# Moving the forget gate's chain of a hybrid recurrent and attention block to 128 rows, earlier in the program

## The chip, the cores and the metric

The kernel runs on one core of a Trainium2 chip. The metric is device time in microseconds for one execution, shown as the median over several. Five engines work side by side, each with its own list of instructions in a fixed order: TensorE (PE in the profile: matrix products), VectorE (DVE) and ScalarE (ACT) for elementwise work, GpSimd (POOL) and SyncE (SP). SP issues the loads of weights; POOL issues a second stream of transfers. An instruction that waits holds up everything behind it on its engine or queue.

## The reference, cut to what matters

A layer of 512 tokens and 1024 channels: a norm, one input projection, a recurrent branch (A), an attention branch with a forget gate (B), a gated sum of both, and a feed-forward part.

```python
h = rms_norm(x, mix_norm_pre[layer])
proj = jnp.einsum("bsd,de->bse", h, w_in[layer])
xa, ga, q, k, v, f_logit, g_a, g_b = jnp.split(proj, offs, axis=-1)
y_a = jax.nn.gelu(ga) * hr                       # hr: the recurrence over xa
y_b = forgetting_attention(q, k, v, f_logit + b_forget[layer])
merged = (jax.nn.sigmoid(g_a + b_merge[layer, 0]) * jnp.einsum("bse,ed->bsd", y_a, w_proj_a[layer])
          + jax.nn.sigmoid(g_b + b_merge[layer, 1]) * jnp.einsum("bse,ed->bsd", y_b, w_proj_b[layer]))
# in forgetting_attention, per head: 16 heads, 512 tokens
cum = jnp.cumsum(jax.nn.log_sigmoid(f_logit.astype(jnp.float32)), axis=1).transpose(0, 2, 1)
sc = sc + cum[:, :, qs:qe, None] - cum[:, :, None, :qe]
```

The forget gate is small: 16 logits per token, their log-sigmoid, and a running sum over the tokens. Attention needs it as a bias on its scores.

## The kernel before, in words

Precision: every product is made of three, with both operands split into a high half (a rounded copy: `wh`, `yh`, `hh`) and a low half (the rest: `wl`, `yl`, `hl`). A weight goes through three steps: SP loads it (`raw_…`), ACT rounds it (`wh_…`, L205), DVE subtracts (`wl_…`, L208). The pool `wpool` has four buffers of each kind. `unit(name)` hands out a weight and starts the ones two further on.

The stages that matter, in the order of TensorE:

- **ga**: ten products of 24 matmuls (`ga0` to `ga9`, function `project`). Their results go through GeLU and times the recurrence to `yh`, `yl` (L800 to L805).
- **pa**: the branch's output projection, sixteen loads and units of 15 matmuls (L251 to L253), here numbered 0 to 15 in the order `PA_ORDER`. Unit 3 is the first that needs the rows of `yh`, `yl` from the second half, the last of them `ga9`'s.
- **q0, k0**: the first query and key projections; then the **gates** `ma`, `mb`, sixteen tiles in eight pairs, with seven products per pair (sums of blocks of weights and activations take the place of an eighth). Their operands are sums over the normed activations: `hf` (L887 to L890), its high half `gsh` (ACT, L967) and low half `gsl` (DVE), and sums of weights `gt` with `gth`, `gtl`.

After each unit, `background` has POOL make a copy of one column of `wh` (`tick`, L182), which places the next of the background transfers (`td`, sums of blocks of the last weight matrix, through HBM) behind that unit. The buffer of `wh` is free for its next weight only when the tick has read it.

The function `forget` is called once, in `early_sums(3)`, so behind pa unit 3: its weights are split (L841 to L845), 16 matmuls make `pf` of 48 rows (L848, L849), ACT and DVE add the bias to `z` (16 rows of 512). `log1p_exp_neg` (L303 to L316) works out the log of 1 + exp(-|z|) by a series: some 14 operations of DVE and one exp on ACT. Then the running sum (`tensor_tensor_scan`, L860), the keys (L862), and four transfers to `cnd` in HBM, from where attention reads them later. Right after, `early_sums(3)` closes the pool of these tiles, and the tiles `hf` are laid into the same memory. `early_sums(6)` to `(11)` make the sums `hf`, `(12)` loads the first gate pair (`raw_ma`), `(13)` to `(15)` make its sums.

Within this part the framework's scheduler keeps the written order where operands allow it and puts ready work between; the later gate part has a schedule written by hand. On SP the loads and the chain's transfers stand in one list.

Of the kernel before, what the change touches and what calls it, by code (L numbers as in the profile page):

```python
# [8 lines left out]
F32 = mybir.dt.float32  # L9
# [3 lines left out]
ALU = mybir.AluOpType  # L13
# [3 lines left out]
P = 128  # L17
S = 512
D = 1024
KD = D // P  # L20
NT = S // P
DR = 1280
TR = DR // P
# [3 lines left out]
H = 16  # L27
# [26 lines left out]
PO = [0, 128, 384, 768, 1280]  # L54
# [43 lines left out]
def kernel(  # L98
# [15 lines left out]
    nc = tc.nc  # L114
    act, dve, pool, pe = nc.scalar, nc.vector, nc.gpsimd, nc.tensor
# [7 lines left out]
    def bank(name):  # L123
        return pspools[-1].tile([P, 512], F32, tag="ps", name=name)
# [55 lines left out]
    def background(n, w):  # L180

        i = pool.tensor_copy(out=tick, in_=w[0].bitcast(F32)[:, 0, 0:1])  # L182
        with tc.issue_after(i.ins):
            for _ in range(n):
                next(transfers, lambda: None)()
# [58 lines left out]
    def unit(name, ahead=2):  # L244

        i = where[name]
        fetch(i + ahead)
        return ready.pop(name)
# [6 lines left out]
    def project(dst, unit, ah, al, lo=0, hi=S):  # L255
        wh, wl = unit
        for k in range(KD):
            mm3(dst[:, lo:hi], wh[:, k], wl[:, k], turns(ah[:, k, lo:hi]), turns(al[:, k, lo:hi]), k == 0, k == KD - 1)
# [60 lines left out]
    mstk = ExitStack()  # L319
# [36 lines left out]
    def sub(out, a, b):  # L356
        dve.tensor_tensor(out=out, in0=a, in1=b, op=ALU.subtract)  # L357
# [173 lines left out]
    with ExitStack() as rg:  # L531
# [242 lines left out]
        def batch(ops):  # L774
            with tc.issue_after(last_act[0].ins):
                for op in ops:
                    last_act[0] = op()
# [8 lines left out]
        def rg_sqrt(t):  # L786
            return lambda: act.activation(out=tt[t], in_=tt[t], func=AF.Sqrt)
# [4 lines left out]
        def scan(t):  # L792
            dve.tensor_tensor(out=tt[t], in0=tt[t], in1=ixt[t], op=ALU.mult)
            dve.tensor_tensor_scan(out=ixt[t], data0=rt[t], data1=tt[t], initial=0.0, op0=ALU.mult, op1=ALU.add)
# [21 lines left out]
                inflow(t)  # L816
        v_out(1, pv)
        steps = {0: (range(0, 4), ()), 1: (range(4, TR), range(0, 2)), 2: ((), range(2, 5)), 3: ((), range(5, 7)), 4: ((), range(7, 9)), 5: ((), range(9, TR))}
        outs = {2: (0,), 3: (1,), 4: (2, 3), 5: (4,), 6: (5,), 7: (6, 7), 8: (8,), 9: (9,)}
        for t in range(TR):  # L820
            gas[t] = bank(f"ga{t}")
            w = unit(f"ga{t}")
            project(gas[t], w, hh, hl)
            background(2, w)
            sq, sc = steps.get(t, ((), ()))
            batch([rg_sqrt(i) for i in sq])
            for i in sc:
                scan(i)
            for i in outs.get(t, ()):
                gate_out(i)  # L830

        papool = mstk.enter_context(tc.tile_pool(name="pa", bufs=1, reuse_waits="tile"))
        pa = papool.tile([P, KD, S], F32, name="pa")
        cnd = ctx.enter_context(tc.tile_pool(name="cnd", bufs=1, space=bass.MemoryType.DRAM)).tile([H, PO[NT]], F32, name="cnd")

        def forget():
            def tl(name, n=H, dt=F32):
                return tpool.tile([P, S], dt, tag="tt", name=f"f_{name}")[0:n]

            fr = tl("fr", P)[:, : KD * H].rearrange("p (k e) -> p k e", k=KD)  # L840
            nc.sync.dma_start(fr, w_f)  # L841
            fw = tl("fw", P, F32R)[:, : KD * 48].rearrange("p (k e) -> p k e", k=KD)
            pool.memset(fw[:, :, H:32].bitcast(F32), 0.0)
            act.copy(fw[:, :, 0:H], fr)
            dve.tensor_tensor(out=fw[:, :, 32:48], in0=fr, in1=fw[:, :, 0:H].bitcast(F32), op=ALU.subtract)  # L845
            pf = bank("f")
            for k in range(KD):
                pe.matmul(pf[0:48], fw[:, k], turns(hh[:, k]), start=k == 0, stop=False)  # L848
                pe.matmul(pf[0:48], fw[:, k], turns(hl[:, k]), start=False, stop=k == KD - 1)  # L849
            z = tl("z")  # L850
            act.copy(z, pf[32:48])
            dve.scalar_tensor_tensor(out=z, in0=pf[0:H], scalar=cpt[0:H, C_BF : C_BF + 1], in1=z, op0=ALU.add, op1=ALU.add)
            with tc.issue_after(last_act[0].ins):
                l1p = log1p_exp_neg(z, tl)
            dve.tensor_scalar(out=z, in0=z, scalar1=0.0, scalar2=None, op0=ALU.min)
            dve.scalar_tensor_tensor(out=z, in0=l1p, scalar=-2.0, in1=z, op0=ALU.mult, op1=ALU.add)
            ones = tl("ones")
            pool.memset(ones, 1.0)
            cum = tl("cum")
            dve.tensor_tensor_scan(out=cum, data0=ones, data1=z, initial=0.0, op0=ALU.mult, op1=ALU.add)  # L860
            keys = tl("keys")
            dve.tensor_scalar(out=placed(keys), in0=parted(cum), scalar1=-8.0, scalar2=None, op0=ALU.mult)  # L862
            for b in range(NT):
                nc.sync.dma_start(cnd[:, PO[b] : PO[b + 1]], keys[:, : PO[b + 1] - PO[b]])

        tgpool = mstk.enter_context(tc.tile_pool(name="tg", bufs=3, reuse_waits="tile"))
        gdram = ctx.enter_context(tc.tile_pool(name="gdram", bufs=1, space=bass.MemoryType.DRAM))
# [6 lines left out]
        fq = []  # L874

        def early_sums(step):
            if step == 3:
                forget()
                rg2.close()
                gates.kpool = dstk.enter_context(tc.tile_pool(name="gkeep", bufs=2, reuse_waits="tile"))  # L880
                gates.tpool = sumstk.enter_context(tc.tile_pool(name="gsum", bufs=2, reuse_waits="tile"))
                hfpool = hfstk.enter_context(tc.tile_pool(name="hf", bufs=1, reuse_waits="tile"))
                fq.extend(hfpool.tile([P, KH, SH], F32, name=f"hf{i}") for i in range(4))
            elif 6 <= step < 10:
                i = step - 6
                k, c = (slice(0, KH), slice(KH, KD))[i % 2], (X, Y)[i // 2]
                dve.tensor_tensor(out=fq[i], in0=hh[:, k, c].bitcast(F32), in1=hl[:, k, c].bitcast(F32), op=ALU.add)  # L887
            elif step == 10:
                dve.tensor_tensor(out=fq[3], in0=fq[2], in1=fq[3], op=ALU.add)
                sub(fq[2], fq[0], fq[2])  # L890
            elif step == 11:
                sub(fq[0], fq[3], fq[0])
                sub(fq[1], fq[1], fq[0])
            elif step == 12:
                gp[0] = Pair(gates, 0, GP[0])
            elif step == 13:
                gp[0].sums(0)
                gp[0].sums(1)
            elif step == 14:
                gp[0].sums_hi(0)  # L900
                gp[0].sums_lo(0)
            elif step == 15:
                gp[0].sums_hi(1)
                gp[0].sums_lo(1)
# [881 lines left out]
```

## Time and profile before

| what | value |
|---|---|
| median of 3 runs | 884.7 us (884.02 to 884.9) |
| the profiled execution's own time | 884.92 us |
| its span in the trace | 883.1 us |
| mean granted clock of TensorE | 0.998 |
| busy: TensorE, VectorE, ScalarE, GpSimd | 868.6, 743.5, 608.4, 236.3 us |
| the 16 f matmuls | 191.2 to 194.7 us |
| the forget chain on VectorE | 195.5 to 215.4 us |
| the four cnd transfers | issued from 215.41 us |
| the sums hf begin | 221.47 us |
| q0 begins on TensorE | 233.53 us |

Times within the execution count from the start of the span. In the rows of the profile a tile's name stands without its number; `out<-in` says what is written from what; a bracket at a row's end gives the idle time before the instruction and what ended it. SPq and POOLq rows are the issues of transfers; in the list of issues the last number is the time from issue to landing.

### The profile page before, as it was taken

To read this page: it belongs to the slowest core of one execution; us is meant where nothing else is said; L and a number is where in the kernel's file an instruction comes from. 1 tells how busy PE (TensorE), PEld (TensorE's weight loads), DVE (VectorE), ACT (ScalarE), POOL (GpSimd) and SP (SyncE) were. 2 spreads that over 40 slices of the span, in tenths; PEclk is the share of its full clock that TensorE was granted. 3 is DMA by queue.
4 is the path that set the end of the run, shared out by engine and by line. 5 is a ranking of instruction groups with operands and counts; after the bars stand their busy time and mean duration, and the time that the engine had idled before them with its cause. 6 is when DMAs were issued, how large, how long until landed. Compare 5 with 4: busy or idle time off the path is not lost.

```text
span 883.1 us, 15782 instructions
## 1 busy us (share of the span) xinstructions
PE 868.6 (98%) x5856; PEld 792.3 (90%) x5856; DVE 743.5 (84%) x1209; ACT 608.4 (69%) x1031; POOL 236.3 (27%) x283
## 2 busy tenths in 40 slices
PE   9999999999999999999999999999999999999996
PEld 7888888888899998888888889999999999888884
DVE  8986479637978849998868599999999999889997
ACT  7565695532466648776754597888888888688774
POOL 4244344535411024232205100242332332100000
PEclk9999999999999999999999999999999999999999
DMA  7787689999865477453506762879899898699864
GB/s 269 242 288 207 188 214 265 227 273 196 190 148 165 120 261 274 133 173 127 203 26 203 234 200 95 192 178 241 210 222 240 209 233 210 230 384 303 280 192 147
DMA packets 71040, 185.24 MB, mean 210 GB/s; under 512 B 7153, under 2 KB 27681, under 8 KB 70578
## 3 DMA queue, kind: packets, MB, share of 16 engines
q1 hardware_dynamic: 47360, 127.72, 43.4%
q0 software_dynamic: 23456, 56.37, 29.8%
q8 instruction: 46, 0.75, 0.3%
q14 instruction: 32, 0.26, 0.1%
q10 hardware_dynamic: 146, 0.14, 0.0%
HBM read 150.69 MB, written 35.73 MB: 211 GB/s over the span
## 4 chain that ended last, share of the span: by engine, by line
PE 83%; DVE 8%; issue 4%; ACT 2%; POOL 2%; DMA 1%; DVEq 0%; ACTq 0%; POOLq 0%
PE up L464 7%; PE up L462 7%; PE up L461 7%; PE dn L1490 2%; PE dn L1488 2%; PE dn L1489 2%; PE ga L252 2%; PE ga L251 2%; PE ga L253 2%; DVE al L357 2%; PE pb L251 2%; PE xa L251 2%; PE v L341 2%; PE xa L253 2%; PE v L342 2%
## 5 line engine op out<-in xcount | busy, mean ns | idle before, releaser
L397 POOL DMA_DIRECT2D ml<-raw_up x42 | 36.1, 859 | 147.6 <-ACT ml L396 82.5
L1360 DVE SCALAR_TENSOR_TENSOR u<-up,cpt,u 128x511 f32<-128x511 f32 x96 | 71.3, 745 | 3.5 <-ACT u L1354 1.8
L1490 PE MATMUL dn<-wh_dn,al 128*128 128x512 f32 (+1 forms) x180 | 66.6, 370 | 1.3 <-DVE al L357 0.7
L1489 PE MATMUL dn<-wl_dn,ah 128*128 128x512 f32 (+1 forms) x180 | 66.1, 367 | 0.5 <-DVE wl_dn L208 0.5
L1488 PE MATMUL dn<-wh_dn,ah 128*128 128x512 f32 (+1 forms) x180 | 65.8, 366 | 0.2 <-ACT ah L1454 0.2
L461 PE MATMUL up<-sh,th 128*128 128x256 f32 x252 | 59.5, 275 | 0.0
L462 PE MATMUL up<-sl,th 128*128 128x256 f32 x252 | 59.5, 275 | 0.0
L208 DVE TENSOR_TENSOR wl_dn<-raw_dn,wh_dn 128x1024 fp32r<-128x1024 f32 x42 | 52.9, 1259 | 5.4 <-ACT wh_dn L205 5.2
L357 DVE TENSOR_TENSOR tl<-t,th 128x1024 fp32r<-128x1024 f32 x42 | 51.1, 1218 | 0.0
L1354 ACT ACTIVATE u<-up,cpt 128x512 f32<-128x512 f32 x48 | 37.0, 778 | 20.1 <-PE up L464 10.0
L205 ACT CAST wh_dn<-raw_dn 128x1024 fp32r<-128x1024 f32 x42 | 44.4, 1058 | 6.1 <-PE dn L1490 3.7
L461 PEld LDWEIGHTS up<-sh,th 128*128 128x128 f32 x252 | 48.4, 192 | 0.0
L462 PEld LDWEIGHTS up<-sl,th 128*128 128x128 f32 x252 | 48.4, 192 | 0.0
L1368 POOL TENSOR_TENSOR yf<-u,u 128x512 f32<-128x512 f32 x23 | 30.5, 1328 | 59.3 <-issue 46.5
L443 ACT CAST th<-t 128x1024 fp32r<-128x1024 f32 x42 | 43.8, 1044 | 2.4
L1490 PEld LDWEIGHTS dn<-wh_dn,al 128*128 128x128 f32 x180 | 34.1, 189 | 8.0 <-DVE al L357 4.1
L955 POOL TENSOR_TENSOR B<-B,mask 128x128 f32<-128x128 f32 x64 | 30.6, 506 | 34.8 <-DMA B<-cnd 33.7
L461 PE MATMUL up<-h2h,mh 128*128 128x256 f32 x168 | 39.7, 275 | 0.0
L462 PE MATMUL up<-h2l,mh 128*128 128x256 f32 x168 | 39.7, 275 | 0.0
L1489 PEld LDWEIGHTS dn<-wl_dn,ah 128*128 128x128 f32 x180 | 34.1, 189 | 5.8 <-DVE wl_dn L208 1.8
L1050 ACT ACTIVATE P<-P,mx 128x384 f32<-128x384 f32 (+3 forms) x64 | 35.2, 552 | 5.3 <-DVE mx L1045 4.3
L464 PE MATMUL up<-sh,tl 128*128 128x256 f32 x252 | 38.4, 275 | 0.0
(731 smaller groups left out, 3252.4 us busy)
## 6 DMA issues: line engine op xcount, KB each, us to landing
raw_up<-in_w_up_dram SPq DMA_DIRECT2D x48, 512.0 KB, 5.5
td<-in_w_down_dram POOLq DMA_DIRECT2D x36, 512.0 KB, 6.3
raw_dn<-td SPq DMA_DIRECT2D x24, 512.0 KB, 5.4
ml<-raw_up POOLq DMA_DIRECT2D x21, 512.0 KB, 5.4
B<-cnd POOLq DMA_DIRECT2D x16, 640.0 KB, 5.7
raw_dn<-in_w_down_dram SPq DMA_DIRECT2D x18, 512.0 KB, 4.4
raw_wo<-in_w_out_dram SPq DMA_DIRECT2D x16, 512.0 KB, 4.4
td<-td POOLq DMA_DIRECT2D x12, 512.0 KB, 11.2
```

The source lines that it names most:

```text
L205: act.copy(self.wh, self.raw)
L208: engine.tensor_tensor(out=self.wl, in0=self.raw, in1=self.wh.bitcast(F32), op=ALU.subtract)
L251: pe.matmul(dst, ah, bh, start=first, stop=False)
L357: dve.tensor_tensor(out=out, in0=a, in1=b, op=ALU.subtract)
L443: act.copy(self.th[i], self.t[i])
L461: pe.matmul(dst, wh[:, k], turns(ah[:, k]), start=first and k == 0, stop=False, skip_group_check=True)
L462: pe.matmul(dst, wh[:, k], turns(al[:, k]), start=False, stop=False, skip_group_check=True)
L464: pe.matmul(dst, wl[:, k], turns(ah[:, k]), start=False, stop=k == KH - 1, skip_group_check=True)
L1360: dve.scalar_tensor_tensor(out=c[:, s:], in0=ps[:, : S - s], scalar=col(C_CFW + 3 * e + j), in1=c[:, s:], op0=ALU.mult, op1=ALU.add)
L1488: pe.matmul(d[:, x], ah[:, k, tok], bh, start=first, stop=False, skip_group_check=True)
L1489: pe.matmul(d[:, x], ah[:, k, tok], bl, start=False, stop=False, skip_group_check=True)
L1490: pe.matmul(d[:, x], al[:, k, tok], bh, start=False, stop=last, skip_group_check=True)
```

## The change

`forget` becomes a generator in pieces, and two tensors in HBM, `zd` and `ld`, are added. The first piece (weights) runs in ga behind `ga5`, the matmuls and `z` behind `ga8`, the next behind `ga9`, the logarithm in `early_sums(1)`, the running sum and the keys in `early_sums(4)`. Between, `z` is written to `zd` and read back as `f_wide`: the same numbers on 128 rows of 64 columns. The series works on these, in four slices of one tile. Its result goes to `ld` and comes back as `f_zl` on 16 rows of 512, since the running sum runs along a row. The sums `hf` and the first gate pair stand one step earlier than before.

```diff
-        for t in range(TR):
-...
+        HC = P // H
+        fdram = ctx.enter_context(tc.tile_pool(name="fdram", bufs=1, space=bass.MemoryType.DRAM))
+        zd, ld = (fdram.tile([H, S], F32, name=n) for n in ("zd", "ld"))
         def forget():
...
             dve.tensor_tensor(out=fw[:, :, 32:48], in0=fr, in1=fw[:, :, 0:H].bitcast(F32), op=ALU.subtract)
+            yield
             pf = bank("f")
...
             dve.scalar_tensor_tensor(out=z, in0=pf[0:H], scalar=cpt[0:H, C_BF : C_BF + 1], in1=z, op0=ALU.add, op1=ALU.add)
-            with tc.issue_after(last_act[0].ins):
-                l1p = log1p_exp_neg(z, tl)
-            dve.tensor_scalar(out=z, in0=z, scalar1=0.0, scalar2=None, op0=ALU.min)
-            dve.scalar_tensor_tensor(out=z, in0=l1p, scalar=-2.0, in1=z, op0=ALU.mult, op1=ALU.add)
+            nc.sync.dma_start(zd, z)
             ones = tl("ones")
             pool.memset(ones, 1.0)
+            yield
+            wide = tl("wide", P).rearrange("p (n c) -> p n c", c=S // HC)
+            parts = {n: wide[:, i] for i, n in enumerate(("z", "y", "d", "s"))}
+            z2 = parts["z"]
+            nc.sync.dma_start(z2, zd.rearrange("h (n c) -> (h n) c", n=HC))
+            yield
+            with tc.issue_after(last_act[0].ins):
+                l1p = log1p_exp_neg(z2, parts.get)
+            dve.tensor_scalar(out=z2, in0=z2, scalar1=0.0, scalar2=None, op0=ALU.min)
+            dve.scalar_tensor_tensor(out=z2, in0=l1p, scalar=-2.0, in1=z2, op0=ALU.mult, op1=ALU.add)
+            nc.sync.dma_start(ld.rearrange("h (n c) -> (h n) c", n=HC), z2)
+            zl = tl("zl")
+            nc.sync.dma_start(zl, ld)
+            yield
             cum = tl("cum")
-            dve.tensor_tensor_scan(out=cum, data0=ones, data1=z, initial=0.0, op0=ALU.mult, op1=ALU.add)
+            dve.tensor_tensor_scan(out=cum, data0=ones, data1=zl, initial=0.0, op0=ALU.mult, op1=ALU.add)
...
+        fg = forget()
+        for t in range(TR):
+...
+            background(2, w)
+            if t in (5, 8, 9):
+                next(fg)
+...
         def early_sums(step):
-            if step == 3:
-                forget()
+            if step == 1:
+                next(fg)
+            elif step == 4:
+                next(fg, None)
                 rg2.close()
...
-            elif 6 <= step < 10:
-                i = step - 6
+            elif 5 <= step < 9:
+                i = step - 5
...
-            elif step == 12:
+            elif step == 11:
                 gp[0] = Pair(gates, 0, GP[0])
-            elif step == 13:
+            elif step == 12:
                 gp[0].sums(0)
                 gp[0].sums(1)
```

How the lists of the engines change is shown at two places. First VectorE around the running sum (`f_cum`), the keys and the sums `hf`. The low halves `wl_pa` before are those of units 13, 14 and 15:

```order
L860 SCALAR_TENSOR_TENSOR f_cum<-f_ones,f_z 16x512
L862 TENSOR_SCALAR f_keys<-f_cum 16x512
L208 TENSOR_TENSOR wl_pa_1_2257<-raw_pa_1_2255,wh_pa_1_2256 128x640
L208 TENSOR_TENSOR wl_pa_0_2284<-raw_pa_0_2282,wh_pa_0_2283 128x640
L887 TENSOR_TENSOR hf_2077<-hh,hl 128x1024
L887 TENSOR_TENSOR hf_2078<-hh,hl 128x1024
L887 TENSOR_TENSOR hf_2079<-hh,hl 128x1024
L887 TENSOR_TENSOR hf_2080<-hh,hl 128x1024
L208 TENSOR_TENSOR wl_pa_1_2311<-raw_pa_1_2309,wh_pa_1_2310 128x640
```

In the change the same stretch of VectorE holds the low halves of units 6 to 11:

```order
L208 TENSOR_TENSOR wl_pa_0_2067<-raw_pa_0_2065,wh_pa_0_2066 128x640
L861 SCALAR_TENSOR_TENSOR f_cum<-f_ones,f_zl 16x512
L208 TENSOR_TENSOR wl_pa_1_2114<-raw_pa_1_2112,wh_pa_1_2113 128x640
L863 TENSOR_SCALAR f_keys<-f_cum 16x512
L208 TENSOR_TENSOR wl_pa_0_2140<-raw_pa_0_2138,wh_pa_0_2139 128x640
L909 TENSOR_TENSOR hf_2108<-hh,hl 128x1024
L909 TENSOR_TENSOR hf_2109<-hh,hl 128x1024
L208 TENSOR_TENSOR wl_pa_1_2164<-raw_pa_1_2162,wh_pa_1_2163 128x640
L909 TENSOR_TENSOR hf_2110<-hh,hl 128x1024
L208 TENSOR_TENSOR wl_pa_0_2190<-raw_pa_0_2188,wh_pa_0_2189 128x640
L909 TENSOR_TENSOR hf_2111<-hh,hl 128x1024
L911 TENSOR_TENSOR hf_2111<-hf_2110,hf_2111 128x1024
```

The running sum now waits for a transfer (`f_zl`) with the low halves of units 7 and later behind it, and the sums `hf` stand ahead of unit 9's low half, where they stood ahead of unit 15's.

Second SP, from the chain's first transfer to the load of unit 10 (loads of units 7, 8, 9 and 10 among them); before, only loads stood here:

```order
L843 DMA zd<-f_z 16x512
L850 DMA f_wide<-zd 128x64
L199 DMA raw_pa_1_2112<-in_w_proj_a_dram 128x640
L199 DMA raw_pa_0_2138<-in_w_proj_a_dram 128x640
L199 DMA raw_pa_1_2162<-in_w_proj_a_dram 128x640
L856 DMA ld<-f_wide 128x64
L858 DMA f_zl<-ld 16x512
L199 DMA raw_pa_0_2188<-in_w_proj_a_dram 128x640
```

Each reading transfer waits on SP until the writing one ahead of it has landed. Further down the list, in the change, the pair `raw_ma` follows the loads of units 12 and 13 and stands ahead of those of units 14 and 15; before, it stood behind unit 14's and ahead of unit 15's.

```order
L199 DMA raw_pa_0_2239<-in_w_proj_a_dram 128x640
L199 DMA raw_pa_1_2264<-in_w_proj_a_dram 128x640
L380 DMA raw_ma_2288<-in_w_in_dram 128x1024
L380 DMA raw_ma_2289<-in_w_in_dram 128x1024
L199 DMA raw_pa_0_2293<-in_w_proj_a_dram 128x640
L199 DMA raw_pa_1_2322<-in_w_proj_a_dram 128x640
L199 DMA raw_q_2347<-in_w_in_dram 128x1024
```

The pair takes the buffers of units 10 and 11; unit 14's load takes that of unit 12, unit 15's that of 13, and q0's that of 14. A load is issued when the low half made from the buffer's last weight is done.

More of the change, by code (lines that the diff above doesn't have):

```diff
@@ L818 @@
         steps = {0: (range(0, 4), ()), 1: (range(4, TR), range(0, 2)), 2: ((), range(2, 5)), 3: ((), range(5, 7)), 4: ((), range(7, 9)), 5: ((), range(9, TR))}
-        outs = {2: (0,), 3: (1,), 4: (2, 3), 5: (4,), 6: (5,), 7: (6, 7), 8: (8,), 9: (9,)}
-        for t in range(TR):
[L821 to L833, printed above, removed]
         cnd = ctx.enter_context(tc.tile_pool(name="cnd", bufs=1, space=bass.MemoryType.DRAM)).tile([H, PO[NT]], F32, name="cnd")
+        HC = P // H
+        fdram = ctx.enter_context(tc.tile_pool(name="fdram", bufs=1, space=bass.MemoryType.DRAM))
+        zd, ld = (fdram.tile([H, S], F32, name=n) for n in ("zd", "ld"))
         def forget():
@@ L864, in forget @@
                 nc.sync.dma_start(cnd[:, PO[b] : PO[b + 1]], keys[:, : PO[b + 1] - PO[b]])
+        fg = forget()
+        outs = {2: (0,), 3: (1,), 4: (2, 3), 5: (4,), 6: (5,), 7: (6, 7), 8: (8,), 9: (9,)}
+        for t in range(TR):
+            gas[t] = bank(f"ga{t}")
+            w = unit(f"ga{t}")
+            project(gas[t], w, hh, hl)
+            background(2, w)
+            if t in (5, 8, 9):
+                next(fg)
+            sq, sc = steps.get(t, ((), ()))
+            batch([rg_sqrt(i) for i in sq])
+            for i in sc:
+                scan(i)
+            for i in outs.get(t, ()):
+                gate_out(i)
+        papool = mstk.enter_context(tc.tile_pool(name="pa", bufs=1, reuse_waits="tile"))
+        pa = papool.tile([P, KD, S], F32, name="pa")
         tgpool = mstk.enter_context(tc.tile_pool(name="tg", bufs=3, reuse_waits="tile"))
@@ L883, in early_sums @@
                 fq.extend(hfpool.tile([P, KH, SH], F32, name=f"hf{i}") for i in range(4))
-            elif 6 <= step < 10:
-                i = step - 6
+            elif 5 <= step < 9:
+                i = step - 5
                 k, c = (slice(0, KH), slice(KH, KD))[i % 2], (X, Y)[i // 2]
                 dve.tensor_tensor(out=fq[i], in0=hh[:, k, c].bitcast(F32), in1=hl[:, k, c].bitcast(F32), op=ALU.add)
-            elif step == 10:
+            elif step == 9:
                 dve.tensor_tensor(out=fq[3], in0=fq[2], in1=fq[3], op=ALU.add)
                 sub(fq[2], fq[0], fq[2])
-            elif step == 11:
+            elif step == 10:
                 sub(fq[0], fq[3], fq[0])
                 sub(fq[1], fq[1], fq[0])
+            elif step == 11:
+                gp[0] = Pair(gates, 0, GP[0])
             elif step == 12:
-                gp[0] = Pair(gates, 0, GP[0])
-            elif step == 13:
                 gp[0].sums(0)
```

## The prediction

> **What bounds the kernel now.** I read the page's first part, then the busy time by stretch, then TensorE's waits, then the timelines of VectorE (DVE), ScalarE (ACT) and the load queue SP around the change, and last how long transfers take to land.
>
> ```profile
> span 883.1 us, 15782 instructions
> PE 868.6 (98%) x5856; PEld 792.3 (90%) x5856; DVE 743.5 (84%) x1209; ACT 608.4 (69%) x1031; POOL 236.3 (27%) x283
> 186.00:215.00 29.00, 29.00 (x136) 24.32 (x136) 20.12 (x27) 10.37 (x16) 16.66 (x18) 1.00 1.00 196
> 215.00:240.00 25.00, 24.14 (x112) 20.84 (x111) 19.11 (x21) 8.66 (x12) 12.07 (x5) 1.00 0.94 207
> 240.00:252.00 12.00, 10.52 (x71) 9.68 (x71) 10.53 (x13) 8.70 (x11) 0.89 (x1) 1.00 0.59 154
> 252.00:300.00 48.00, 48.00 (x432) 48.00 (x431) 40.81 (x58) 31.77 (x53) 5.09 (x6) 1.00 0.57 155
> PE q L253 <- DVE wl_q L208: 0.9, 1, 0.9
> PE ma L461 <- DVE ma L480: 1.5, 1, 1.5
> ```
>
> TensorE (the first number after the stretch's length) is busy 98% of the span at a granted clock of 1.00 in these stretches. Where the forget chain runs today, 186 to 215, it does not idle at all. It idles only behind it: 0.9 us at the first q projection and 1.5 us at the first gate product, 2.3 us together. No change to this stretch can win more than that, 0.27%; from 252 on TensorE is full again.
>
> ```profile
> 213.68 1.21 DVE L860 TENSOR_TENSOR_SCAN f_cum<-f_ones,f_z 16x512 f32<-16x512 f32 x1
> 214.93 0.45 DVE L862 TENSOR_SCALAR f_keys<-f_cum 16x512 f32<-16x512 f32 x1
> 221.47 4.63 DVE L887 TENSOR_TENSOR hf<-hh,hl 128x1024 f32<-128x1024 f32 x4 [2.52 <-DMA cnd<-f_keys]
> 233.71 1.22 DVE L208 TENSOR_TENSOR wl_q<-raw_q,wh_q 128x1024 fp32r<-128x1024 f32 x1
> 229.04 8.20 POOL L182 COPY tick<-wh_pa 128x1 f32<-128x1 f32 x1
> 237.28 1.04 ACT L205 CAST wh_k<-raw_k 128x1024 fp32r<-128x1024 f32 x1 [2.33 <-POOL tick L182]
> 238.70 3.89 ACT L967 CAST gsh<-hf 128x1024 fp32r<-128x1024 f32 x4
> 250.19 0.43 DVE L480 TENSOR_TENSOR ma<-ma,gx 128x256 f32<-128x256 f32 x1 [1.44 <-ACT gx L468]
> ```
>
> The reader is to see one chain: the norm's sums hf start 6.1 us after the keys are done, because their memory is that of the keys, which the four cnd transfers still read. They fill DVE until wl_q at 233.71, so q waits. The tick, a copy on POOL, needs 8.2 us beside them and holds wh_k, hence gsh at 238.70, hence the add at 250.19 on which the gate product waits.
>
> **The change, part by part.** TensorE's work is the same; the sixteen f matmuls only move from behind pa unit 3 to behind ga8.
>
> ```profile
> 178.28 0.38 PE L251 MATMUL pa<-yh,wh_pa 128*128 128x512 f32 x1
> 233.53 0.38 PE L251 MATMUL q<-hh,wh_q 128*128 128x512 f32 x1
> 173.10 0.38 PE L251 MATMUL ga<-hh,wh_ga 128*128 128x512 f32 x1
> L848 PE MATMUL f<-hh,f_fw x8: 379/379/379, 191.2 to 194.3; 128*48 128x512 f32 x8
> 195.49 0.74 DVE L852 SCALAR_TENSOR_TENSOR f_z<-f,cpt,f_z 16x512 f32<-16x512 f32 x1 [2.65 <-ACT f_z L851]
> ```
>
> From 178.28 to 233.53 stand 256 matmuls of 0.216 us: a pa unit of 15 is 3.24, f is 3.45. With f first, f runs from 173.10 to 176.55, unit i (0 to 15) starts at 181.73 + 3.24 i, and q at 233.5 as now. z is ready 5.0 us after f's start (196.23 less 191.2): at 178.1.
>
> DVE saves work: twelve operations of 0.68 us and a reciprocal of 3.34 become operations on 64 columns.
>
> ```profile
> L315 DVE SCALAR_TENSOR_TENSOR lp_y_sp<-lp_y_sp,lp_d_sp x7: 155/164/201, 26.0 to 31.7; 128x10 f32<-128x10 f32 x7
> L315 DVE SCALAR_TENSOR_TENSOR f_y<-f_y,f_d x7: 673/680/697, 205.9 to 210.8; 16x512 f32<-16x512 f32 x7
> L309 DVE RECIPROCAL lp_d_sp<-lp_d_sp x1: 218/218/218, 24.0 to 24.0; 128x10 f32<-128x10 f32 x1
> L309 DVE RECIPROCAL f_d<-f_d x1: 3342/3342/3342, 198.1 to 198.1; 16x512 f32<-16x512 f32 x1
> L208 DVE TENSOR_TENSOR wl_pa<-raw_pa,wh_pa x16: 748/821/826, 166.5 to 226.0; 128x640 fp32r<-128x640 f32 x16
> L205 ACT CAST wh_pa<-raw_pa x16: 721/724/728, 165.7 to 223.2; 128x640 fp32r<-128x640 f32 x16
> ```
>
> On a straight line between 10 and 512 columns one is 0.22 us, the reciprocal 0.55. That saves some 10 us of DVE, worth nothing by itself: TensorE waited for none of it (29.00 of 29.00). What counts is that hf comes earlier, and that DVE now stands still in two new places. It can afford little: the low half wl of unit i is made when unit i-4 has left its slot, so DVE has about 3 units less 1.6 us, some 8 us of lead, and unit i needs it 0.43 us after its start (third matmul).
>
> The four new transfers and the four cnd ones go through SP's queue, among the weight loads. How long do they take?
>
> ```profile
> 41.46 0.43 SPq L199 DMA_DIRECT2D raw_v<-in_w_in_dram  x1
> raw_v<-in_w_in_dram SPq DMA_DIRECT2D x1, 512.0 KB, 8.3
> 41.98 0.56 SPq L579 DMA_DIRECT2D halo_h<-xh  x1
> halo_h<-xh SPq DMA_DIRECT2D x1, 32.0 KB, 8.0
> halo_h<-xh SPq DMA_DIRECT2D x1, 32.0 KB, 1.9
> cnd<-f_keys SPq DMA_DIRECT2D x1, 32.0 KB, 4.6
> raw_pa<-in_w_proj_a_dram SPq DMA_DIRECT2D x16, 320.0 KB, 6.1
> 174.74 0.33 SPq L199 DMA_DIRECT2D raw_pa<-in_w_proj_a_dram  x1
> raw_pa<-in_w_proj_a_dram SPq DMA_DIRECT2D x1, 320.0 KB, 8.4
> raw_ma<-in_w_in_dram SPq DMA_DIRECT2D x1, 512.0 KB, 7.0
> raw_ma<-in_w_in_dram SPq DMA_DIRECT2D x1, 512.0 KB, 6.2
> raw_q<-in_w_in_dram SPq DMA_DIRECT2D x1, 512.0 KB, 6.3
> raw_k<-in_w_in_dram SPq DMA_DIRECT2D x1, 512.0 KB, 5.2
> ```
>
> The last number of an issue row is the time to landing. A halo of 32 KB issued at 41.98 landed 8.0 us later, 0.2 behind the load issued before it (41.46 + 8.3 = 49.76): small transfers land in the queue's order. Alone (issued at 76.55) one took 1.9. So a small transfer costs 1.9 us at least, 4.6 by the nearest row of its kind (cnd), and as much as the load ahead of it where there is one; alone but beside the background transfers (DMA share 1.00 in 186 to 215) I take 3.2, the middle.
>
> [...]
>
> Now the walk. zd is issued at 178.15 behind the load of 174.74, which landed at 183.1: 183.1 (at best 180.1). wide then, nothing ahead of it: 186.3. While DVE waits, the last yl and unit 4's wl stand behind it, and exp holds four wh on ACT; all within the lead. Up to ld's source come 14 small operations and exp, taken as one more (3.3), the reciprocal (0.55), and yl, wl 4 and wl 5 (2.1, since yl runs beside exp): 192.3. ld is issued behind the loads of units 8 and 9, the latter issued at 191.6: 197.7, ld 197.9. zl: 201.2.
>
> The scan (1.2), wl 7 (0.8) and the keys (0.45) end at 203.7; unit 7 starts at 204.4, not late. hf starts 6.1 us behind the keys as now, 209.8; two hf (2.3) and wl 9 (0.8) end at 212.9, and unit 9 needs it at 211.3: **1.6 us lost.** Two more hf, their sum, and wl 10 and 11 take 5.0: 217.9. Only then the second raw_ma has a slot (its load, moved one step forward, stands before units 14 and 15): 6.6 us, the mean of 7.0 and 6.2, make 224.5. Three gate sums of half hf's size (1.8) wait for it and wl 13 (0.8) behind them: 227.1, needed at 225.9 with the loss so far: **1.2 lost.** Unit 15's load waits for wl 13's slot; at raw_k's 5.2 it lands at 232.4, wh and wl make 233.9, needed at 233.6: **0.3 lost.** raw_q has wl 14's slot at 229.8 and lands after 6.3 at 236.1; wh_q and wl_q (1.04, 1.22) end at 238.4, q starts at 236.6 and needs it at 237.1: 1.3 instead of 0.85, **0.45 lost.** wh_k no longer waits for a tick but for raw_k (239.1): wh_k starts 1.4 us before gsh as now (237.28, 238.70), so gsh at 240.5, and the add ends 11.9 us later as now (250.6 less 238.7), at 252.4. TensorE gets there at 236.6 + 1.3 + 10.4 (q and k, 48 matmuls) + 3.9 (three products of 12 matmuls half as wide) = 252.2: the 1.5 idle shrinks to 0.2, **1.3 gained.** Sum: 1.6 + 1.2 + 0.3 + 0.45 - 1.3 = +2.25 us. Span 885.35; the profiled run (884.92) would be 887.2; it lies 0.2 above the median, so 887.0 beside 884.7.
>
> The bounds: with every small transfer at 1.9 nothing is late and 2.3 is gained; with unit 9's load at 8.4 (2.3 more), zl at 4.6 (1.4 more), raw_ma at 7.0 (0.4 more), the loss is 6.3.
>
> **Rivals.** *Small transfers land at once.* If ld and cnd take 1.9 us whatever is ahead, ld's source is ready at 191.6 (ACT's table load, not wide, then ends last), zl lands at 195.6, the keys at 198.1, hf starts at 201.4, before wl 9 could be made. Every later load then has its slot when wl is made on time, wl_q is early, gsh starts right at 234: both idles go, 884.7 - 2.3 = 882.4, faster. It decides itself at hf: a start by 207.0 is enough to lose nothing at unit 13. The isolated halo speaks for it, the halos and cnd behind loads against.
>
> [...]
>
> *One loss, one gain.* If hf starts by 208.2, unit 9 is on time, but raw_ma still needs wl 11's slot (216.3): 1.2 lost at unit 13, 0.3 at 15, 0.4 at q, 1.3 gained: +0.6, 885.3. For it: my walk misses it by only 1.6 us.
>
> *Loaded queue.* If the loads ahead of ld and cnd take 8.4 as at 174.74, the upper bound: 891.0. For it: DMA share 1.00 there; against: the median of 6.1.
>
> **How the numbers follow.** Forecast 0.52, own range 885.2 to 889.5; at once 0.16; one loss 0.17; loaded 0.15. A measurement of this kernel (884.02 to 884.9) can tell about 0.2%, 1.8 us, from no change. Slower by more: 0.36 of the forecast and the loaded case, 0.51. Within: 0.16 of the forecast and 0.16 of one loss, 0.32. Faster: at once and 0.01, 0.17. The range 882.5 to 890.3 leaves out 0.1 at each end.
>
> **What would show it.** Right: TensorE waits on wl_pa (at unit 9, then 13) that do not exist now; hf with a wait on cnd of 4 us or more; the scan on zl standing from about 194 to 201; zl and cnd landing just behind weight loads; wh_k no longer behind a tick. Wrong: hf starting before 207, no wait on wl_pa, q and ma without idle; or ticks of many microseconds that hold wh_pa, which I have at nothing because DVE now has gaps.

## The result, and the profile after

The change makes the kernel slower by 0.44%: 888.8 us as median (886.9 to 889.3) beside 884.7 (882.8 to 885.9) on the same chip, ratio 1.0044 with a 95% interval of 1.0034 to 1.0054. The profiled execution took 889.16 us, its span is 887.4. The prediction was 887.0, with 882.5 to 890.3 as the range. The ratios leave out two single executions far above the others of their kernel, one of e9 (994 us) and one of e12 (3203 us).

The first part of the page of the changed kernel:

```profile
span 887.4 us, 15790 instructions
PE 870.0 (98%) x5856; PEld 792.9 (89%) x5856; DVE 734.5 (83%) x1209; ACT 607.9 (69%) x1031; POOL 220.2 (25%) x283
```

Its busy time where the forget chain ran before (after the length: TensorE, weight loads, VectorE, ScalarE, GpSimd, granted clock, share of the DMA engines, GB/s):

```profile
186.00:215.00 29.00, 26.67 (x123) 22.70 (x121) 10.46 (x25) 9.21 (x15) 9.52 (x16) 1.00 1.01 202
```

VectorE has 9.0 us less to do in all (734.5 instead of 743.5), as the change intends. But from 186 to 215, where TensorE was busy 29.00 of 29.00 us before, it now stands for 2.3 us, and VectorE, with 10.46 us of work instead of 20.12, stands too. What TensorE waits for in this part of the program:

```profile
PE pa L253 <- DVE wl_pa L208: 4.5, 2, 3.1
PE q L253 <- DVE wl_q L208: 0.3, 1, 0.3
PE ma L461 <- DVE ma L480: 0.2, 1, 0.2
```

Two waits on low halves of pa units, 4.5 us, that did not exist; the idles at q and at the first gate product are down from 0.9 and 1.5 to 0.3 and 0.2. (A further gate product now waits 0.3 us for a transfer of GpSimd's, `gml`.) VectorE's timeline shows why the low halves are late:

```profile
205.29 1.21 DVE L861 TENSOR_TENSOR_SCAN f_cum<-f_ones,f_zl 16x512 f32<-16x512 f32 x1 [10.30 <-DMA f_zl<-ld]
206.43 0.79 DVE L208 TENSOR_TENSOR wl_pa<-raw_pa,wh_pa 128x640 fp32r<-128x640 f32 x1
214.01 2.36 DVE L909 TENSOR_TENSOR hf<-hh,hl 128x1024 f32<-128x1024 f32 x2 [5.72 <-DMA cnd<-f_keys]
216.29 0.82 DVE L208 TENSOR_TENSOR wl_pa<-raw_pa,wh_pa 128x640 fp32r<-128x640 f32 x1
```

The running sum stands 10.30 us for `f_zl` with the low half of unit 7 (206.43) right behind it, and `hf` stands 5.72 us for `cnd` with that of unit 9 (216.29) behind two sums. The transfers, from the list of issues between 192 and 212 (the last number is the median time to landing):

```profile
q0 software_dynamic: 3127, 3.11, 97.6%
raw_pa<-in_w_proj_a_dram SPq DMA_DIRECT2D x4, 320.0 KB, 5.6
ld<-f_wide SPq DMA_DIRECT2D x1, 32.0 KB, 6.4
f_zl<-ld SPq DMA_DIRECT2D x1, 32.0 KB, 4.5
cnd<-f_keys SPq DMA_DIRECT2D x1, 8.0 KB, 5.4
```

The software queue, which carries the background transfers `td`, fills 97.6% of the sixteen DMA engines' time there.

**How much each place costs** is read better from the starts of matmuls than from the wait rows, since a wait row comes out shorter than what the starts show. First the idle at q of the kernel before, then the one at unit 9 of the changed kernel:

```profile
233.75 0.38 PE L252 MATMUL q<-hl,wh_q 128*128 128x512 f32 x1
234.98 0.48 PE L253 MATMUL q<-hh,wl_q 128*128 128x512 f32 x1 [0.85 <-DVE wl_q L208]
235.30 0.38 PE L251 MATMUL q<-hh,wh_q 128*128 128x512 f32 x1
```

```profile
213.64 0.38 PE L252 MATMUL pa<-yl,wh_pa 128*128 128x512 f32 x1
217.16 0.48 PE L253 MATMUL pa<-yh,wl_pa 128*128 128x512 f32 x1 [3.15 <-DVE wl_pa L208]
217.48 0.38 PE L251 MATMUL pa<-yh,wh_pa 128*128 128x512 f32 x1
```

Matmuls of 512 columns start 0.22 us apart in this part of both kernels where nothing waits. At q the third started 1.23 behind the second and the fourth 0.32 behind it: 1.11 lost, where the row says 0.85. Worked out so for each place:

| place | lost before | lost after | difference | predicted |
|---|---|---|---|---|
| unit 7 | 0 | 1.60 | +1.60 | 0 |
| unit 9 | 0 | 3.40 | +3.40 | +1.6 |
| unit 13 | 0 | 0 | 0 | +1.2 |
| unit 14 | 0 | 0.40 | +0.40 | 0 |
| unit 15 | 0 | 0 | 0 | +0.3 |
| q | 1.11 | 0.58 | -0.53 | +0.45 |
| gate product, waiting for the add | 1.75 | 0.44 | -1.31 | -1.3 |
| gate product, waiting for `gml` | 0 | 0.61 | +0.61 | 0 |
| sum | 2.86 | 7.03 | **+4.17** | **+2.25** |

The sum, from one execution of each kernel, comes close to the difference of the medians (4.1). The spans differ by 4.3; 0.94 of that is a later start-up of this one execution (the first transposes at 8.54 instead of 7.60 us, and anywhere from 0 to 0.94 later in the profiles below, whatever the kernel), and 0.8 comes back behind the gates.

So one question is settled by the trace, where the time goes; open is what makes small transfers so late, and which of the waits matters.

### The profile page after: what moved, and what is told of

It reads as the page before. It is cut to its first block, busy times and chain, and to the rows that moved or that the text cites. A ratio compares the mean times of both kernels' runs of the same rounds, so it can differ in the third digit from the quotient of the medians.

```text
span 887.4 us, 15790 instructions
## 1 busy us (share of the span) xinstructions
PE 870.0 (98%) x5856; PEld 792.9 (89%) x5856; DVE 734.5 (83%) x1209; ACT 607.9 (69%) x1031; POOL 220.2 (25%) x283
## 4 chain that ended last, share of the span: by engine, by line
PE 73%; DVE 12%; DMA 7%; issue 5%; ACT 2%; POOL 1%; SPq 0%; DVEq 0%; ACTq 0%; POOLq 0%
PE up L464 7%; PE up L461 7%; PE up L462 7%; DVE wl_dn L208 2%; DVE al L357 2%; PE ga L251 2%; PE ga L252 2%; PE ga L253 2%; PE pb L251 2%; PE v L341 2%; PE xa L251 2%; PE xa L252 2%; PE v L342 2%; PE xa L253 2%; PE v L343 2%
## 5 line engine op out<-in xcount | busy, mean ns | idle before, releaser
L205 ACT CAST wh_pa<-raw_pa 128x640 fp32r<-128x640 f32 x16 | 11.5, 723 | 39.4 <-DMA raw_pa<-in_w_proj_a_dram 24.9
```

The costliest lines, as they stand in the source:

```text
L205: act.copy(self.wh, self.raw)
```

## The experiments

Four theories at the start. **A**: the loss is VectorE standing still for the chain's transfers, with low halves queued behind. **Q**: the transfers are late because they land behind weight loads of their queue, as the prediction held. **L**: they are late because the DMA engines are loaded. **D**: the new place of the sums `hf` is what costs. All ratios are to the kernel before, run beside on the same chip.

### e1: early, but on 16 rows, without the four transfers

```diff
-            nc.sync.dma_start(zd, z)
...
-            wide = tl("wide", P).rearrange(...)
-            nc.sync.dma_start(z2, zd.rearrange(...))
...
-            nc.sync.dma_start(ld.rearrange(...), z2)
-            nc.sync.dma_start(zl, ld)
...
-            dve.tensor_tensor_scan(out=cum, data0=ones, data1=zl, ...)
+            dve.tensor_tensor_scan(out=cum, data0=ones, data1=z, ...)
```

> The change with everything in its new place, but the series on 16 rows of 512 as before, and so without zd, f_wide, ld and f_zl. Theory A (the loss is VectorE standing still for f_zl and cnd, with the low halves of units 7 and 9 queued behind): z is ready near 179, the long series and the low halves between take some 19 us, so the running sum ends near 200 instead of 206.5, cnd lands before 207, TensorE does not wait on wl_pa at unit 7 and at most 0.5 us at unit 9, and the gain at q and the first gate product stays: 883.0 to 884.5 where before is 884.7, ratio 0.998 to 1.000. Rival B (the 10 us of work that VectorE saves on 128 rows are what the early place needs): the low halves of units 4 to 7 come late behind operations of 0.68 and 3.34 us, TensorE waits on wl_pa there, ratio 1.004 or more.

Measured: 885.4 us, ratio 1.0005 (0.9996 to 1.0014). VectorE's timeline of this kernel:

```profile
201.36 1.21 DVE L853 TENSOR_TENSOR_SCAN f_cum<-f_ones,f_z 16x512 f32<-16x512 f32 x1
209.22 3.50 DVE L901 TENSOR_TENSOR hf<-hh,hl 128x1024 f32<-128x1024 f32 x3 [5.38 <-DMA cnd<-f_keys]
```

And TensorE's waits in this part (us in total, times, longest):

```profile
PE ma L461 <- DVE ma L480: 0.8, 1, 0.8
PE q L253 <- DVE wl_q L208: 0.6, 1, 0.6
PE pa L253 <- DVE wl_pa L208: 0.2, 1, 0.2
```

The series with its operations of 0.68 and 3.34 us lets the running sum start 3.9 us earlier than the short series with its transfers (201.36 against 205.29; 3.5 once the start-up of each execution is taken off), and the waits on `wl_pa` are gone but for 0.2. That speaks for A and against rival B: the 10 us of saved work are not what the early place needs. `hf` still waits 5.38 us for `cnd`, and of the idles at q and at the gate product 0.6 and 0.8 us are left; the time is that of the kernel before, just above what A expected (885.4 us, where 883.0 to 884.5 was said).

### e2: the keys in memory of their own

```diff
-            keys = tl("keys")
+            keys = pa[0:H, PA_ORDER[-1][0]]
```

> The change with the keys in memory that the sums hf do not take over (the last 512 columns of the branch's result, written only at unit 15), so that hf waits for no cnd transfer. Theory A: the wait of 5.7 us ahead of hf goes, with it the 3.15 us at unit 9; the 1.35 us at unit 7 stay, since f_zl is as late as before: 3 us less than the change, ratio 0.9995 to 1.002. Rival C (TensorE waits because the weight loads of units 7 to 10 themselves come late behind the chain's transfers on SP): no difference to the change, ratio 1.0035 to 1.0055.

Measured: 892.6 us, ratio 1.0083 (1.0070 to 1.0097), worse than the change, where A had expected 3 us better. The wait for `cnd` did go, and unit 9's with it; what took its place, first on VectorE's timeline:

```profile
229.54 0.69 DVE L357 TENSOR_TENSOR gt<-raw_ma,raw_ma 128x512 f32<-128x512 f32 x1 [8.88 <-DMA raw_ma<-in_w_in_dram]
```

The transfer it waits for, from the issues between 216 and 222:

```profile
raw_ma<-in_w_in_dram SPq DMA_DIRECT2D x2, 512.0 KB, 9.4
```

And TensorE's timeline behind it:

```profile
232.95 0.79 PE L253 MATMUL pa<-yh,wl_pa 128*128 128x512 f32 x1 [4.20 <-DVE wl_pa L208]
233.54 0.63 PE L251 MATMUL pa<-yh,wh_pa 128*128 128x512 f32 x1
233.96 0.63 PE L252 MATMUL pa<-yl,wh_pa 128*128 128x512 f32 x1
```

VectorE, no longer held at `hf`, made the low halves of units 10 to 12 within 3.5 us, the loads of both `raw_ma` and of unit 14 were issued within 2.6 us, and each took 9.3 to 10.4 us. The gate sums waited 8.88 us for the second `raw_ma` with the low half of unit 13 behind them: the prediction's loss at unit 13, which the wait at unit 9 ahead of it had hidden in the change. And the stalls cost more than their length: behind them matmuls start 0.43 us apart instead of 0.22, eight behind unit 7's (1.99 us here) and twelve behind unit 13's, 4.2 us in all. The last section comes back to that. Rival C falls too: unit 9's wait went while the loads of units 7 to 10 came when they come in the change.

### e3: the sums and the gate pair back one step

```diff
-            elif 5 <= step < 9:
-                i = step - 5
+            elif 6 <= step < 10:
+                i = step - 6
...  (the four following steps likewise)
```

> The change with the sums hf and the first gate pair one step later, at the steps that they have before the change. Theory A: f_zl and cnd are as late as in the change, so unit 7 still waits 1.35 us; at unit 9 one sum of 1.2 us instead of two stands ahead of the low half, so about 2.0 us instead of 3.15; with the sums later by one low half q stays within 0.5 us of the change: ratio 1.002 to 1.004. Rival D (the place of the sums is what costs): both waits on wl_pa go or fall under 0.5 us, ratio 0.998 to 1.000.

Measured: 888.6 us, ratio 1.0043 (1.0030 to 1.0055): no difference to the change. Unit 7 waits 2.05 us, with seven slow matmuls behind it (1.5 us); unit 9 no longer waits, and units 12 and 14 wait 0.47 and 0.52. Rival D falls: where the sums stand by one step moves the stalls and not the time. A had expected 1.002 to 1.004 and unit 9 to wait still.

### e4: ld, f_zl and cnd on a queue without loads

```diff
-            nc.sync.dma_start(ld.rearrange("h (n c) -> (h n) c", n=HC), z2)
+            nc.scalar.dma_start(ld.rearrange("h (n c) -> (h n) c", n=HC), z2)
...  (f_zl and cnd likewise)
```

> The change with ld, f_zl and the four cnd transfers issued by ScalarE, on a queue that holds no weight load; zd and f_wide stay on SP. Theory Q (a small transfer lands only behind the load issued before it on its queue): ld takes about 2 to 3 us instead of 6.4, f_zl 2 to 3 instead of 4.5, cnd 2 to 3 instead of 5.3; the running sum starts near 199, hf near 204; no wait on wl_pa over 0.3 us, ratio 0.998 to 1.000. Rival L (the memory is loaded by all transfers together, whatever their queue): the three take what they take in the change, within 1 us, TensorE waits on wl_pa for 3 us or more, ratio 1.003 to 1.0055.

Measured: 889.3 us, ratio 1.0054 (1.0042 to 1.0067). The issues of this kernel between 192 and 212:

```profile
q0 software_dynamic: 2088, 2.07, 66.6%
ld<-f_wide ACTq DMA_DIRECT2D x1, 32.0 KB, 6.0
f_zl<-ld ACTq DMA_DIRECT2D x1, 32.0 KB, 4.1
cnd<-f_keys ACTq DMA_DIRECT2D x1, 8.0 KB, 2.6
```

Alone on its queue `ld` takes 6.0 us instead of 6.4, `f_zl` 4.1 instead of 4.5. The DMA engines are as full meanwhile: from 194 to 201 us their share is 1.19 here and 1.21 in the change. Q falls for these two: the load ahead was not what they waited for. `cnd`, which falls into a gap of the background transfers in this execution (share 0.42 from 207 to 213), takes 2.6. Units 7 and 8 wait only some 0.5 us each and unit 9 none, but the gate sums again wait for `raw_ma` (3.62 us), and unit 13 waits 2.80.

### e5 and e6: without the adding background transfers

```diff
-            return lambda: nc.gpsimd.dma_start(td[t][m], src, accum_op=ALU.add, max_dma_last_dim=D)
+            return lambda: quiet[0] or nc.gpsimd.dma_start(td[t][m], src, accum_op=ALU.add, max_dma_last_dim=D)
...
             gas[t] = bank(f"ga{t}")
+            quiet[0] = t >= 7
```

e5 is the changed kernel with this edit, e6 the kernel before.

> The change without the adding background transfers (td) from ga7 on: 15 transfers of 512 KB through HBM are left out, so blocks of the last weight matrix are not summed; everything else stands as in the change. Theory L (the DMA engines are filled by these transfers, and everything on any queue waits for them): ld and f_zl take 5.5 us or less together instead of 10.9, cnd 3 or less, raw_ma 5 or less; no wait on wl_pa over 0.3 us; ratio to before 0.997 to 0.9995. Rival Q (a small transfer waits for the load issued before it on SP): raw_pa is still ahead of ld and cnd, which take 5 us or more, the waits on wl_pa stay over 2 us, ratio 1.002 or more.

> The kernel before, without the same 15 background transfers. Theory L: only what they do without the change: cnd lands some 2 us sooner, the sums hf with it, the idle at q (0.9) goes and that at the first gate product (1.5) shrinks to under 0.8: 883.0 to 884.2, ratio 0.998 to 0.9995; what e5 gains on the change over and above this is the loss by transfers of the change's own. Rival: the two idles come from VectorE's work alone and stay as they are, ratio 0.9995 to 1.0005.

Measured: e5 882.0 us, ratio 0.9959 (0.9947 to 0.9972); e6 882.0 us, ratio 0.9958 (0.9945 to 0.9970). Without these transfers the change costs nothing and gains nothing. The stretch from 178 to 215 of the changed kernel, then the same stretch of e5:

```profile
178.00:215.00 37.00, 34.67 (x160) 29.71 (x158) 12.62 (x29) 11.86 (x19) 10.72 (x18) 1.00 0.98 225
```

```profile
178.00:215.00 37.00, 37.00 (x173) 32.41 (x172) 24.60 (x40) 12.30 (x20) 7.65 (x11) 1.00 0.35 111
```

The issues of e5 between 192 and 212:

```profile
raw_pa<-in_w_proj_a_dram SPq DMA_DIRECT2D x4, 320.0 KB, 2.8
raw_ma<-in_w_in_dram SPq DMA_DIRECT2D x2, 512.0 KB, 3.4
ld<-f_wide SPq DMA_DIRECT2D x1, 32.0 KB, 2.2
f_zl<-ld SPq DMA_DIRECT2D x1, 32.0 KB, 1.7
```

And the running sum on its VectorE:

```profile
196.28 1.21 DVE L862 TENSOR_TENSOR_SCAN f_cum<-f_ones,f_zl 16x512 f32<-16x512 f32 x1 [2.50 <-DMA f_zl<-ld]
```

With the DMA engines 0.35 busy instead of 0.98, `ld` and `f_zl` take 3.9 us together instead of 10.9, on the same queue and behind the same loads; the running sum starts 9 us earlier, and TensorE waits nowhere in this part. L holds: the background transfers are what makes these small ones late. (The edit also frees GpSimd from issuing them; it is the landing times that speak for L.) e6 shows that the two idles of the kernel before go with the same transfers: both are gone there, and `hf` starts at 218.89 instead of 221.47, without a wait for `cnd`. It gained more than expected (0.42%, some 3.5 us, where up to 0.2% was): the two idles went altogether, and by the starts of matmuls they cost 2.86; what the rest is, isn't shown.

### e7: keys apart, gate sums behind the low half of unit 13

```diff
-            keys = tl("keys")
+            keys = pa[0:H, PA_ORDER[-1][0]]
...
-                gp[0].sums(0)
-                gp[0].sums(1)
+                with tc.issue_after(lows["pa%d_%d" % PA_ORDER[13]].ins):
+                    gp[0].sums(0)
+                    gp[0].sums(1)
```

`lows` keeps the instruction that makes each low half.

> As e2 (keys in memory of their own), and the first gate pair's four sums held behind the low half of unit 13 on VectorE. Theory G (in e2 the low half of unit 13 was late only because the sums that wait for raw_ma stand ahead of it): the 4.2 us at unit 13 go, at most 1 us comes up at unit 14, the 2.0 us at unit 7 stay: ratio 1.0025 to 1.005 instead of 1.0083. Rival W (the loads themselves come in a bunch behind the standstill, whatever the order on VectorE): waits on wh_pa or wl_pa of units 13 to 15 add up to 3 us or more, ratio 1.006 or more.

Measured: 888.0 us, ratio 1.0032 (1.0022 to 1.0042), within what G expected. The 4.5 us less than e2 come from the order of VectorE's list: the second `raw_ma` is still waited for (7.12 us), but unit 13's low half stands ahead of the wait, and with no stall over 1.4 us there are no slow matmuls either. Left are unit 7 (1.38), unit 10 (0.65), unit 14 (0.30).

### e8: all three: 16 rows early, keys apart, gate sums behind

The edits of e1 and of e7 together:

```diff
-            nc.sync.dma_start(zd, z)
...
+            keys = pa[0:H, PA_ORDER[-1][0]]
...
+                with tc.issue_after(lows["pa%d_%d" % PA_ORDER[13]].ins):
```

> The chain early on 16 rows without the four transfers (as e1), keys in memory of their own (as e2), gate sums behind the low half of unit 13 (as e7). Theory A (what cost was VectorE standing still for small transfers): nothing on VectorE waits for a transfer of the chain any more, hf begins near 203, no wait on wl_pa over 0.3 us, q under 0.6, the first gate product under 0.5: 882.6 to 884.0, ratio 0.9975 to 0.9995, faster than before and than e1 (1.0005). Rival W: q and the gate product wait for raw_q and raw_ma as in e1, 1.0 us or more together, ratio 0.9995 to 1.0015.

Measured: 881.7 us, ratio 0.9961 (0.9949 to 0.9974), better than both kernels and than expected. Two stretches of this kernel:

```profile
186.00:215.00 29.00, 29.00 (x137) 25.38 (x136) 28.62 (x34) 9.01 (x15) 18.69 (x17) 1.00 0.93 199
215.00:244.00 29.00, 29.00 (x136) 25.41 (x135) 17.13 (x19) 14.49 (x18) 5.38 (x7) 1.00 0.96 215
```

The start of `hf` on its VectorE:

```profile
202.62 2.36 DVE L902 TENSOR_TENSOR hf<-hh,hl 128x1024 f32<-128x1024 f32 x2
```

TensorE is busy throughout with the background transfers in place: `hf` begins right behind the keys, 18.9 us earlier than in the kernel before. VectorE is busy 28.62 of 29.00 us, with the long series that the change set out to shorten.

### e9: the change, with what waits held behind what is needed

```diff
-            elif step == 4:
-                next(fg, None)
+            elif step == 6:
+                with behind(8):
+                    next(fg, None)
...
+                with behind(9):
+                    dve.tensor_tensor(out=fq[i], in0=hh[...], in1=hl[...], op=ALU.add)
...
+                with behind(13):
+                    gp[0].sums(0)
+                    gp[0].sums(1)
```

`behind(i)` places an instruction behind the low half of unit i on its engine. The sums `hf` also move, from steps 5 to 8 to steps 7 to 10.

> The change with all its transfers on 128 rows, background transfers and the keys' memory as they are, but on VectorE the running sum held behind the low half of unit 8, the sums hf behind that of unit 9 and the gate sums behind that of unit 13; the gate pair's load stays in its place. Theory A (a transfer costs by what is queued behind the instruction that waits for it): f_zl and cnd land as late as in the change (near 205 and 213), but no low half of a unit that is needed soon stands behind them: waits on wl_pa under 1 us in total, ratio 0.999 to 1.002. Rival W (late transfers bunch the loads, whatever the order): waits on wl_pa or wh_pa of 2 us or more at units 10 to 15, ratio 1.003 or more.

Measured: 886.7 us, ratio 1.0015 (1.0006 to 1.0024). The running sum on VectorE:

```profile
204.76 1.21 DVE L862 TENSOR_TENSOR_SCAN f_cum<-f_ones,f_zl 16x512 f32<-16x512 f32 x1 [5.23 <-DMA f_zl<-ld]
```

TensorE's longest waits of this part:

```profile
PE ma L465 <- DMA gml<-raw_ma: 1.6, 1, 1.6
PE pa L252 <- ACT wh_pa L205: 1.0, 1, 1.0
PE ma L462 <- DVE ma L481: 0.8, 1, 0.8
PE pa L254 <- DVE wl_pa L208: 0.8, 2, 0.6
```

`f_zl` lands about when it did (204.64; 205.16 in the change), yet nothing at units 7 and 9 is late: two thirds (1.0015 instead of 1.0044) of the loss were the order and not the transfers' time. The rest is spread: 1.8 us at units 11 and 14, and at the gates the add is waited for 0.8 us and `gml`, a transfer that GpSimd issues, 1.6.

### e10: the 128 rows alone, in the old place

The kernel before with only `forget`'s body exchanged for that of the change:

```diff
+            nc.sync.dma_start(zd, z)
...
+            nc.sync.dma_start(z2, zd.rearrange("h (n c) -> (h n) c", n=HC))
...
+            nc.sync.dma_start(ld.rearrange("h (n c) -> (h n) c", n=HC), z2)
+            nc.sync.dma_start(zl, ld)
```

> The kernel before, with only the series moved to 128 rows of 64 (with zd, f_wide, ld, f_zl) in the old place behind pa unit 3; sums hf and gate pair at their old steps. Theory A: four transfers of 3 to 6 us each make some 18 us of waiting where the narrow series saves 10 us of work; keys near 221 instead of 215, hf near 227, low halves of late units and wl_q behind them: TensorE loses 3 us or more, ratio 1.004 to 1.012. Rival B (the saved work pays): ratio 1.000 or less.

Measured: 893.3 us, ratio 1.0093 (1.0075 to 1.0110). The running sum on VectorE:

```profile
222.14 1.21 DVE L872 TENSOR_TENSOR_SCAN f_cum<-f_ones,f_zl 16x512 f32<-16x512 f32 x1 [9.11 <-DMA f_zl<-ld]
```

And TensorE's waits behind it:

```profile
PE pa L253 <- DVE wl_pa L208: 3.5, 2, 3.3
PE q L253 <- DVE wl_q L208: 2.1, 1, 2.1
```

The running sum starts 8.5 us later than on 16 rows in the same place (213.68). So of the change's two halves it is the 128 rows that cost: 0.93% in the old place, 0.44% in the early one. The early place alone, on 16 rows, neither costs nor gains (e1, 1.0005).

### e12 and e13: whose gain is e8's

e12 is e8 without the keys' own memory; e13 is the kernel before with nothing but the keys' own memory:

```diff
-            keys = tl("keys")
+            keys = pa[0:H, PA_ORDER[-1][0]]
```

> As e8, but the keys in the memory that hf takes over, so hf waits for cnd as in e1 (5.4 us). If the keys' memory is what made e8 faster than e1: hf near 209, waits at q and the first gate product of 0.8 us or more together, ratio 0.9990 to 1.0010. If the order of the gate sums did: as e8, ratio 0.995 to 0.9975.

> The kernel before with only the keys moved to memory that hf does not take over. If the idle at q (0.9) and at the first gate product (1.5) comes from hf waiting for cnd: hf starts near 215.5 instead of 221.5, wl_q is made before q, gsh is early, both idles go: ratio 0.9965 to 0.9985. If it comes from the loads of the last weights beside the background transfers: ratio 0.999 to 1.0005.

Measured: e12 884.8 us, ratio 0.9997 (0.9988 to 1.0006); e13 882.6 us, ratio 0.9970 (0.9960 to 0.9980). First a row of e12, then one of e13:

```profile
208.92 3.50 DVE L902 TENSOR_TENSOR hf<-hh,hl 128x1024 f32<-128x1024 f32 x3 [5.44 <-DMA cnd<-f_keys]
```

```profile
216.34 4.63 DVE L887 TENSOR_TENSOR hf<-hh,hl 128x1024 f32<-128x1024 f32 x4
```

The single edit of e13, one line, gives 0.30% of e8's 0.39%. In its profiled execution, the slowest of its runs (884.3 us), TensorE has one wait left in this part:

```profile
PE ma L461 <- DVE ma L480: 1.2, 1, 1.2
```

The idle at q is gone and that at the gate product is 1.2 instead of 1.5; how short the latter is in its median run isn't shown. Whether e8's early place adds anything to it isn't settled: the two intervals overlap. Without the keys' own memory the early place gives nothing (e12: `hf` waits 5.44 us for `cnd`, and 1.1 and 0.6 us are lost at q).

## Why the prediction was right, and where it was not

- **That it gets slower, by waits on `wl_pa`, with the idles behind it shrinking**: right. Two waits on low halves (at units 7 and 9, where 9 and 13 were said), `hf` standing 5.72 us (4 or more was said), the running sum standing from 195 to 205 (194 to 201 was said), no tick ahead of `wh_k` (the longest on `wh_pa` takes 1.49 us, where one took 8.20 before). Of the forms the loss could take, it named the right one and put 2.25 us on it; it was 4.17. That the sum came as near as it did owes something to luck: terms that were too small by 4.4 us together (units 7, 9 and 14, `gml`) stand against terms too large by 2.5 (units 13 and 15, q). And the range of 882.5 to 890.3 also held a faster kernel, so that the time lies in it says little.
- **Durations on VectorE**: right. The straight line between 10 and 512 columns gave 0.22 us for an operation on 64 columns and 0.55 for the reciprocal; they took 0.18 to 0.23 and 0.55.
- **The walk up to ld's source**: 192.3 said; 193.3 measured once the 0.94 us of start-up are taken off. `zd` took 5.7 us (5.0 said), `f_wide` 3.3 (3.2 said).
- **"zl: 201.2"**: the step that failed, by the size of its terms. `f_zl` landed at 204.2 on the same count, 3.0 us late: 1.0 came in with ld's source, 0.8 by `ld` (6.4 instead of 5.6) and 1.2 by `f_zl`, for which 3.2, the middle between 1.9 and 4.6, was taken and 4.5 came out. The reason for choosing the middle, that a small transfer with no load ahead of it is quick, is what e4 contradicts: with no load on its queue `ld` took 6.0. From this step unit 7 was late by 1.60 where nothing was said, and unit 9 by 3.40 instead of 1.6.
- **"Small transfers land in the queue's order"**: not what made them slow. The halo rows that the prediction leaned on fit loaded DMA engines as well: their share is 0.78 from 42 to 50 us, where a halo took 8.0, and 0.22 from 76 to 79, where one took 1.9. On a queue of its own `ld` still took 6.0 us, 0.4 less than in the change, beside DMA engines as full (share 1.19 and 1.21); with the same queue and no background transfers, 2.2.
- **Rival "small transfers land at once", 882.4**: its condition is met in e5, by leaving out the background transfers, and nothing is late there: 882.0. But e6 takes 882.0 without the change, so the nearness of the two numbers doesn't confirm the rival's sum; in the change itself its condition failed. The rival's 1.9 us is near the 2.2 and 1.7 that `ld` and `f_zl` took in e5, and not near the 6.4 and 4.5 that they took in the change.
- **Unit 13, 1.2 us**: not there in the change, since unit 9 had lost 3.40 already and everything behind it had that much more time. The mechanism was right and came up at 4.2 us as soon as unit 9 was helped (e2), and at 2.8 (e4).
- **Unit 15, 0.3 us**: nothing was lost there; 0.40 was lost at unit 14, which the prediction didn't name.
- **q, 0.45 lost**: the wrong sign, 0.53 gained; `raw_q` was predicted to land after 6.3 us and took 4.6.
- **"No change to this stretch can win more than 2.3"**: too low a ceiling. By the starts of matmuls the two idles cost 2.86, and the wait rows were 0.5 short of that. e8 wins 0.39%, 3.4 us (2.3 to 4.5 by its interval).

## What to carry to other kernels

Ask of a change that trades arithmetic for a round trip through memory what the transfers take in that stretch, beside what fills the DMA engines there (1.7 us and 4.5 us for the same 32 KB here), and not what they take alone; in e10, ten microseconds of saved work on an engine that isn't the bound bought fifteen of waiting on it (6.08 for `f_wide`, 9.11 for `f_zl`). Look at what stands behind an instruction that will wait, on its own engine: two thirds of this loss went by moving three such instructions behind work that was needed sooner, and a single line that stopped two tiles from sharing memory gained 0.30%, where the whole change lost 0.44%. When one stall is removed, look for the next resource that is then asked for in a bunch: e2 did what it should and cost 0.39% more than the change.

## What the runs showed of the hardware that was not expected

**A stall of TensorE can cost more than its length.** The stretch behind e4's stall of 2.80 us, with the granted clock as the last number but two:

```profile
230.00:232.00 2.00, 2.00 (x5) 1.64 (x6) 0.69 (x1) 0.00 (x0) 0.02 (x1) 0.50 1.25 200
```

Its matmuls, two at the start and the first that follows at full speed:

```profile
230.59 0.63 PE L251 MATMUL pa<-yh,wh_pa 128*128 128x512 f32 x1
231.02 0.63 PE L252 MATMUL pa<-yl,wh_pa 128*128 128x512 f32 x1
233.06 0.38 PE L251 MATMUL pa<-yh,wh_pa 128*128 128x512 f32 x1
```

The granted clock is 0.50 from 230 to 232, and matmuls start 0.43 us apart, until some 3 us behind the stall. Starts 0.43 us apart also show behind stalls of 1.99 and 4.20 us (e2: eight and twelve slow matmuls), 2.05 (e3: seven), 3.32 and 2.09 (e10: ten and seven); each slow matmul costs 0.21 us. They do not show behind the stall of 3.15 us at unit 9 of the changed kernel (217.48 above is followed by starts 0.22 apart), nor behind that of 1.62 in e9 or any shorter one in this part. So stalls of 1.99 to 2.09 us were enough here and one of 3.15 was not: length alone doesn't decide. The prediction had no term for this, and that the change escaped it was luck: why it did the runs don't show, and e3 and e4 lost a further 1 to 2 us behind their stalls.

**Background transfers slow the loads too, not only the small transfers.** A load of 320 KB took 5.6 us beside them in the changed kernel and 2.8 in e5; one of 512 KB took 9.4 in e2, with three loads under way together, and 3.4 in e5. Which part of the way to memory is shared, the DMA engines or the memory, the runs don't tell.
